# A two-layer streaming encoder step: an earlier selection of the tile whose gates are added in DRAM, and 94 blocks of scores made ahead instead of 82

## The chip, the core and the metric

The kernel runs on one core of one Trainium2 chip. The metric is the device time of one execution in microseconds (us); the kernel before took 4004.89 us, the median of three runs from 3994.92 to 4011.67. Engines are named as in the profile: PE is TensorE's matmul, PEld its weight load, DVE is VectorE, ACT ScalarE, POOL GpSimd, SP SyncE. SP issues the plain transfers and POOL the indirect ones.

## The reference

One inference step of two layers over 640 tokens: 512 of a prompt and 128 of running streams (the sample). Each layer is a token mixer followed by an expert retrieval (PEER) with 16384 experts, each a row of a table `u` and of a table `v`. Per block of 128 tokens:

```python
q = (xb @ w_query).reshape(TB, 8, 2, 128)
s = einsum('thpd,hpkd->thpk', q, keys)
sv, si = top_k(s, 16)
cand = sv[:, :, 0, :, None] + sv[:, :, 1, None, :]
cv, ci = top_k(cand.reshape(TB, 8, 256), 16)
gate = softmax(cv)
act = gelu(einsum('thkd,td->thk', u_tab[idx], xb), approximate=False)
y = einsum('thk,thkd->td', gate * act, v_tab[idx])
```

So each token meets 8 x 16 = 128 experts; `idx` is the expert's row, `gate` its weight.

## The kernel before, in words

The kernel does the retrieval in two ways. The **sparse** way (`sparse_peer`, L852) gathers the 128 chosen rows of `u` and then of `v` for 128 tokens, one row per token and gather, by 256 indirect transfers from POOL (L880, L913), and reduces them on DVE (L884, L920). In each layer it serves the sample and the first of the prompt's four tiles of 128 tokens (the first tile, `GT`). The **dense** way (`dense_peer`, L974) serves the other three tiles, 384 tokens: it makes the scores of all 16384 experts in 128 blocks of 128 experts, multiplies them with a matrix of gates that is zero where an expert was not chosen, and adds up `v`. A block has two halves on PE: 24 matmuls of 384 columns for its scores (8 chunks of the model dimension, 3 products of split float32) and 18 matmuls of 512 columns that combine the gated scores with `v` (L1122, in `combine`). Gelu is on ACT (L996, L1101), the product with the gates on DVE (L1110).

Since the gates are known late, some scores are made ahead: `ahead` (L985) loads a block of `u` (tile `wraw`, L272 in `halves`, two buffers), splits it on ACT and DVE (`whi` L240, `wlo` L241), multiplies, and stores the scores after gelu in DRAM (`sd`, L997). They are the last blocks: with 82 made ahead the loop makes the scores of blocks 0 to 45 itself (L284, in `product2`) and reads those of 46 to 127 back from `sd` (L1096).

The gates of the three tiles come about in two ways. For two tiles `found` (L999) builds them from one-hot matrices on DVE, ACT and PE (L1017 to L1046) and stores them to DRAM as `gd` (L1049), 4 pieces a tile. For the other one, in layer 1 only, `spread` (L1052) adds them in DRAM, into a zeroed array `gz`, by 128 indirect transfers (L1070) of 128 elements each, in 8 groups of 16. In front of each group and behind the last stands a small memset on POOL (`stone`, L1063), the fence: it waits until all 16 transfers of the group before have landed. The loop reads `gz` four blocks at a time (`gch`, L1105), and this load waits for the last fence; it stands in SP's queue with all other plain transfers.

What is selected for a tile is worked out by `select` (L805): some 60 DVE operations from `cand` (L815) over the top 16 to the index tile (`idf`, L865, for the first tile; `at0` and `ati`, L1056 to L1059, for the spread tile).

`FE[l]` holds three numbers for layer l: how many blocks are made ahead during the routing (12), how many at each of the 8 pieces of `found`, and how many in all. The program's order is that of the code at the end of the main function (L1239 to L1275); `de` is the generator of the dense way, and each `next(de)` runs it to its next `yield`. A scheduler then sets each engine's own order from the program and a simulated time line, so a moved piece of code moves rows on all engines.

Of the kernel before, what the change touches and what calls it, by code (L numbers as in the profile page):

```python
# [24 lines left out]
GM, GR, GS = ((4,),(1,)*40+(2,)*60), (8,8), (8,8)  # L25
# [20 lines left out]
SUM = dict(s=(None, "xn"), t=("vm", "vm"))  # L46
KQ = (-1, -1)
SC = (0, 1)
FE = ((12, 5, 72), (12, 8, 82))


class Group:
# [10 lines left out]
def kernel(ctx: ExitStack, tc: tile.TileContext, t: dict):  # L63
# [12 lines left out]
    def tl(tag, shape, dt=F32, name=None):  # L76
        return sb.tile(shape, dt, name=name or tag, tag=tag, bufs=BUFS.get(tag, 1))
# [7 lines left out]
    def gps(who):  # L85
        turn[who] = turn.get(who, -1) + 1
        return bank(banks[who][turn[who] % len(banks[who])])
# [85 lines left out]
    def cleared():  # L173

        while mark[0] is None:
            yield 1
        after(V.memset(zero, 0.0))
        flat = gz.rearrange("g p k t -> (g p k t)").rearrange("(p r c) -> p r c", p=128, c=256)
        for i in range(0, 64, 16):
            fills.append(Y.dma_start(flat[:, i:i + 16], zero[:, None].to_broadcast([128, 16, 256])))  # L180
            for _ in range(6):
                yield 1
# [669 lines left out]
    def sparse_peer(G, l, xhl, sv, si, quad, acc=None):  # L852


        who = G.name
        xn = tl("xn", [128, 1024], name="xnn")
        for hf in range(2):
            p = gps(who)
            for u in range(4):
                for v in range(2):  # L860
                    T.matmul(p[:, 128 * u:128 * u + 128], xhl(v, 4 * hf + u), identr, start=(v == 0), stop=(v == 1))
            S.activation(xn[:, 512 * hf:512 * hf + 512], p, AF.Copy)
        k1, k2, gate = select(who, sv, si, quad)
        idf = tl("idf", [128, 128])
        V.scalar_tensor_tensor(idf, k1, 128.0, k2, op0=OP.mult, op1=OP.add)  # L865
        idt = None
        if acc is None:
            tp = gps(who)[:, :128]
            T.transpose(tp, idf, ident)
            idt = tl("bt", [128, 128], I32, name="idt")  # L870
            V.tensor_copy(idt, tp)
        yield 1
        idx = tl("bi", [128, 128], I32, name="idx")
        after(V.tensor_copy(idx, idf))  # L874
        w = tl("wact", [128, 128])
        rows = []
        for s in range(128 + LG):
            if s < 128:
                rows.append(tl("g", [128, 1024], name="gu"))
                P.indirect_dma_start(out=rows[s], out_offset=None, in_=t["u"][l],  # L880
                                     in_offset=bass.IndirectOffsetOnAxis(ap=idx[:, s:s + 1], axis=0))
            if s >= LG:
                g = rows[s - LG]
                d = V.tensor_tensor_reduce(out=g, in0=g, in1=xn, scale=1.0, scalar=0.0, op0=OP.mult, op1=OP.add,  # L884
                                           accum_out=w[:, s - LG:s - LG + 1])
                if paced[0] == 2:
                    after(d, 4 - s % 4)
                elif s % 4 == 0 and paced[0]:
                    after(d)
            yield 1  # L890
        S.activation(w, w, AF.Gelu)
        V.tensor_tensor(w, w, gate, op=OP.mult)
        if acc is not None:
            yield from weighted(G, l, idx, w, acc)
        else:
            yield from multiplied(G, l, idt, w)
# [77 lines left out]
    def dense_peer(l, xhl, sv, si):  # L974

        G = GA
        n = G.n
        FIRST, EACH, NA = FE[l]
        AHEAD = list(range(128 - NA, 128))
# [176 lines left out]
    def after(ins, back=0):  # L1156

        m = marks[-back] if back and len(marks) >= back else mark[0]
        if m is not None:
            tc.add_manual_dep(ins.ins, m.ins.name, mybir.DependencyInfo(  # L1160
                mybir.DependencyClass.NoSync, mybir.DependencyReason.SCHED_ONLY), reason="order")
# [3 lines left out]
    def gather(n):  # L1165
        for _ in range(n):
            at = tc.cur_priority
            tc.cur_priority = at + later[0]
            while gathers:
                try:  # L1170
                    next(gathers[0])
                    break
                except StopIteration:
                    gathers.pop(0)
            tc.cur_priority = at
# [18 lines left out]
    def mixer_p(l):  # L1194
        if l == 0:
            mixt = [tl("v4", [128, 2, 512], name=f"mix{i}") for i in range(4)]
            yield from even_p(mixt)
        else:
            yield from hgrn(GP, GsP([tl("v4", [128, 2, 512], name=f"gs{i}") for i in range(4)]))
# [10 lines left out]
    for l in range(2):  # L1210
        if l:
            tg["p"].update(sq="w3", r="ge", v="ge", a="g8")
            banks.update(WB)
        order = iter(ORDER[l])
        clears = cleared() if SC[l] else iter(())
        mp = mixer_p(l)
        mk, mark[0], paced[0] = 0, None, THR[0]
        later[0] = LW[l]
        while True:
            w = next(order, "P")  # L1220
            next(clears, None)
            if w == "S":
                if cs is not None:
                    next(cs, None)
                continue
            if next(mp, None) is None:
                break
            if gathers:
                gather(GM[l][mk % len(GM[l])])
                mk += 1  # L1230
                if l and mk == PS:
                    banks["p"] = ["y0", "y1", "s"]
        for _ in clears:
            pass
        for _ in cs or ():
            pass
        paced[0] = False
        later[0] = LATER
        xhl = rmsnorm(GP, 1 + 2 * l)  # L1239
        banks.update({"p": ["y0", "y1", "y2", "y3"], "a": ["y0", "y1", "y2", "y3"], "h": ["s", "y5"]})  # L1240
        sv, si = tl("v4", [128, 4, 16, 16], name="sv"), tl("w3", [128, 4, 16, 16], U16, name="si")
        xa = lambda v, k, xhl=xhl: xhl(v, k)[:, 128:512]
        xt = lambda v, k, xhl=xhl: xhl(v, k)[:, 0:128]
        de = dense_peer(l, xa, sv[:, 1:4], si[:, 1:4])
        for i, _ in enumerate(route_p(l, xhl, sv, si)):
            if i < FE[l][0]:
                next(de)
            gather(GR[l])
        spt = sparse_peer(GT, l, xt, sv[:, 0], si[:, 0], "v4", SUM["t"][l])
        next(spt)  # L1250
        if KT[l] < 0:
            gathers.append(spt)
        for i in range(12 - 4 * SC[l]):
            next(de)
            if i == KQ[l]:
                gathers.append(spt)
            gather(GS[l])
        mark[0], paced[0] = None, THR[1 + l]
        marks.clear()
        later[0] = LD[l]  # L1260
        if l == 0:
            banks.update({"s": ["s"], "u": ['b']})
            tg["s"] = dict(w=[SW1], sq="sq", r="pa", v="pb", a="idf", x="pa")
            cs = chain_s(1)
        for k, _ in enumerate(de):
            if k == KT[l]:
                gathers.append(spt)
            if l or gathers and (gathers[0] is spt or cs is not None):
                gather(PACE[l][k % len(PACE[l])])
            if l == 0 and cs is not None and k >= K0:  # L1270
                if spt not in gathers:
                    tg["s"]["w"] = SW2
                    banks["s"] = SB2
                    if late and next(late[0], None) is None:
                        late.pop(0)  # L1275
                for _ in range(SN[k % len(SN)]):
                    if cs is not None and next(cs, None) is None:
                        cs = None
        if l == 0:
            while late:  # L1280
                for _ in late.pop(0):
                    pass
            for _ in cs or ():
                pass
            cs = None
        paced[0] = False
        later[0] = LATER
        while gathers and (l or gathers[0] is spt):
            gather(1)
# [78 lines left out]
```

## Time and profile before

| | |
|---|---|
| runs before, median (lowest to highest) | 4004.89 us (3994.92 to 4011.67) |
| profiled execution, its own time | 4018.61 us |
| its span in the profile | 4016.7 us |
| busy share PE, PEld, DVE, ACT, POOL | 89%, 73%, 80%, 41%, 40% |
| chain that ended last, by engine | PE 22%, DVE 12%, DMA 10%, POOL 6% |
| transfers over the span | 1097.66 MB, 273 GB/s |

A profile is one execution. Views of it name a group of equal instructions by line, engine and tiles (out<-in), with count and times in microseconds from the span's start. Layer 1's routing ends near 2870 us; the pieces of `found` and the blocks ahead run until 3219 us, the dense loop of layer 1 from 3272 us to the end.

### The profile page before, as it was taken

The page shows a single profiled execution, that of the slowest core. Times are in us where ns is not written, and L with a number is a line of the kernel's source. Part 1 is how long each engine was busy: PE and PEld are TensorE (multiplying, and loading weights), DVE is VectorE, ACT ScalarE, POOL GpSimd, SP SyncE. Part 2 cuts the span into 40 slices and gives each one's busy share as a digit, 9 for nine tenths or more (in the row PEclk, how much of TensorE's full clock was granted, in tenths as well). Part 3 has the DMA queues.
Part 4 walks back from the last instruction along what each step waited for, and adds up shares of the span by engine and source line. Part 5 has one row for each costly group of instructions (what it writes and reads, how often), then busy time and mean ns, then how long its engine had stood idle before and what let it go on. Part 6 is the DMA issues. An engine that isn't in the chain of part 4 may idle for free.

```text
span 4016.7 us, 51334 instructions
## 1 busy us (share of the span) xinstructions
PE 3567.8 (89%) x17676; PEld 2921.1 (73%) x17676; DVE 3217.4 (80%) x6206; ACT 1655.5 (41%) x2717; POOL 1596.2 (40%) x1173
## 2 busy tenths in 40 slices
PE   6978778999999999788998878787999949999998
PEld 4756666789779997556775555566999949998776
DVE  5558999886568879887679877899998738788898
ACT  6644222467633334334444333231348913333333
POOL 0001665431245555541003553564057764444443
PEclk8989899999999999999999777798999979999999
DMA  4334998886789999998665765688457769999999
GB/s 147 113 110 160 328 338 322 317 326 241 264 298 336 338 333 357 370 362 304 227 230 216 258 235 186 225 321 296 140 164 211 211 177 343 334 337 356 385 385 331
DMA packets 480134, 1097.66 MB, mean 273 GB/s; under 512 B 55537, under 2 KB 260337, under 8 KB 474737
## 3 DMA queue, kind: packets, MB, share of 16 engines
q1 hardware_dynamic: 313984, 557.38, 39.7%
q0 software_dynamic: 165888, 537.01, 37.9%
q8 instruction: 139, 2.28, 0.2%
q14 instruction: 123, 1.00, 0.1%
HBM read 1005.92 MB, written 89.23 MB: 273 GB/s over the span
## 4 chain that ended last, share of the span: by engine, by line
PE 22%; DVE 12%; DMA 10%; POOL 6%; issue 5%; ACT 1%; SPq 0%; DVEq 0%; POOLq 0%; ACTq 0%
PE py L1122 10%; POOL gz L1070 5%; DMA ge<-sd 4%; DMA gu<-u,idx 3%; PE ps L284 2%; DVE wlo L241 2%; DVE yv L920 2%; PE pb L284 2%; PE py L291 1%; PE py L292 1%; PE py L293 1%; DMA gz<-gatea,ati 1%; DVE gu L884 1%; PE ps L312 1%; DMA wraw<-v 1%
## 5 line engine op out<-in xcount | busy, mean ns | idle before, releaser
L240 ACT ACTIVATE whi<-wraw 128x1024 fp32r<-128x1024 f32 x710 | 741.3, 1054 | 1024.5 <-PE py L292 307.6
L241 DVE TENSOR_TENSOR wlo<-wraw,whi 128x1024 fp32r<-128x1024 f32 x710 | 862.0, 1217 | 315.1 <-ACT whi L240 124.9
L880 POOL DMA_INDIRECT gu<-u,idx x512 | 670.4, 1309 | 1028.5 <-DVE idx L874 380.1
L1122 PE MATMUL py<-whi,wt 128*128 128x512 f32 x3072 | 798.8, 405 | 107.4 <-ACT wt L240 90.6
L1122 PEld LDWEIGHTS py<-whi,wt 128*128 128x128 f32 x3072 | 581.5, 192 | 258.9 <-ACT wt L240 102.3
L913 POOL DMA_INDIRECT gv<-v,idx x384 | 522.0, 1359 | 540.6 <-DVE yv L920 357.0
L884 DVE CUSTOM_DVE_ANT_0 gu<-gu,xnn 128x1024 f32<-128x1024 f32 x512 | 616.2, 1218 | 58.2 <-DMA gu<-u,idx 57.0
L291 PE MATMUL py<-xhl,whi 128*128 128x512 f32 (+1 forms) x1344 | 522.5, 389 | 74.5 <-ACT xhl L240 30.8
L293 PE MATMUL py<-xhl,wlo 128*128 128x512 f32 (+1 forms) x1344 | 515.9, 385 | 26.6 <-DVE wlo L241 26.3
L292 PE MATMUL py<-xhl,whi 128*128 128x512 f32 (+1 forms) x1344 | 514.1, 382 | 11.1 <-DVE xhl L241 11.0
L920 DVE SCALAR_TENSOR_TENSOR yv<-gv,wact,yv 128x1024 f32<-128x1024 f32 x381 | 486.7, 1277 | 2.7
L1122 PE MATMUL py<-wlo,wt 128*128 128x512 f32 x1536 | 401.6, 393 | 0.7 <-DVE wlo L241 0.7
L291 PE MATMUL ps<-xhl,whi 128*128 128x384 f32 (+1 forms) x1120 | 387.2, 346 | 7.9 <-ACT sm L510 3.7
L293 PE MATMUL ps<-xhl,wlo 128*128 128x384 f32 (+1 forms) x1120 | 388.5, 347 | 3.6 <-DVE wlo L241 3.4
L292 PE MATMUL ps<-xhl,whi 128*128 128x384 f32 (+1 forms) x1120 | 385.1, 344 | 0.0
L291 PEld LDWEIGHTS py<-xhl,whi 128*128 128x128 f32 x1344 | 264.6, 197 | 133.7 <-ACT xhl L240 35.1
L1122 PEld LDWEIGHTS py<-wlo,wt 128*128 128x128 f32 x1536 | 288.6, 188 | 67.6 <-DVE wlo L241 1.3
L1070 POOL DMA_INDIRECT gz<-gatea,ati x128 | 249.2, 1947 | 202.6 <-DVE mr L771 162.1
L293 PEld LDWEIGHTS py<-xhl,wlo 128*128 128x128 f32 x1344 | 264.4, 197 | 84.9 <-DVE wlo L241 37.7
L292 PEld LDWEIGHTS py<-xhl,whi 128*128 128x128 f32 x1344 | 264.8, 197 | 46.8 <-DVE xhl L241 15.1
L944 POOL DMA_INDIRECT gv<-v,idt x128 | 151.7, 1185 | 324.5 <-PE pb L962 296.3
L291 PEld LDWEIGHTS ps<-xhl,whi 128*128 128x128 f32 x1120 | 213.9, 191 | 21.3 <-ACT ge L996 5.8
(444 smaller groups left out, 4947.0 us busy)
## 6 DMA issues: line engine op xcount, KB each, us to landing
wraw<-uT SPq DMA_DIRECT2D x256, 512.0 KB
wraw<-v SPq DMA_DIRECT2D x256, 512.0 KB
wraw<-w SPq DMA_DIRECT2D x98, 512.0 KB
gd<-st SPq DMA_DIRECT2D x40, 1024.0 KB
wraw<-wq SPq DMA_DIRECT2D x64, 512.0 KB
sd<-ge SPq DMA_DIRECT2D x154, 192.0 KB
gch<-gd SPq DMA_DIRECT2D x32, 768.0 KB
ge<-sd SPq DMA_DIRECT2D x114, 192.0 KB
```

The lines of the kernel that those rows point to most:

```text
L240: S.activation(hi, src, AF.Copy)
L241: return V.tensor_tensor(lo, src, hi.bitcast(F32), op=OP.subtract)
L284: m = T.matmul(p, w[wv][:, k], xhl(xv, k), start=(k == 0 and xv == wv), stop=(k == 7 and wv == 1))
L291: T.matmul(p, w[0][:, k], xhl(0, k), start=(k == 0), stop=False)
L292: T.matmul(p, w[0][:, k], xhl(1, k), start=False, stop=False)
L293: T.matmul(p, w[1][:, k], xhl(0, k), start=False, stop=(k == 7))
L880: P.indirect_dma_start(out=rows[s], out_offset=None, in_=t["u"][l], in_offset=bass.IndirectOffsetOnAxis(ap=idx[:, s:s + 1], axis=0))
L884: d = V.tensor_tensor_reduce(out=g, in0=g, in1=xn, scale=1.0, scalar=0.0, op0=OP.mult, op1=OP.add, accum_out=w[:, s - LG:s - LG + 1])
L913: P.indirect_dma_start(out=rows[s], out_offset=None, in_=t["v"][l], in_offset=bass.IndirectOffsetOnAxis(ap=idx[:, s:s + 1], axis=0))
L920: d = V.scalar_tensor_tensor(y, rows[e], w[:, e:e + 1], y, op0=OP.mult, op1=OP.add)
L1070: d = P.indirect_dma_start(out=flat, out_offset=bass.IndirectOffsetOnAxis(ap=ati[:, j:j + 1], axis=0), in_=gate[:, j:j + 1], in_offset=Non ...
L1122: mult[1] = T.matmul(yp[a][hf], wt[:, wv, 128 * a:128 * a + 128], vh[vv][:, 512 * hf:512 * hf + 512], start=(k == 0 and wv == 0 and vv == ...
```

## The change

In layer 1 the generator `de` is run once more in front of `sparse_peer` for the first tile, so `spread` (its selection and 128 indirect transfers) and the first piece of `found` now stand in the program ahead of the first tile's selection; the loop behind has one step less. The middle number of `FE[1]` goes from 8 to 10 and the last from 82 to 94: at the 8 pieces 10 blocks each are made ahead, the last call makes the 2 that are left, and the dense loop makes the scores of 34 blocks itself instead of 46.

```diff
-FE = ((12, 5, 72), (12, 8, 82))
+FE = ((12, 5, 72), (12, 10, 94))
...
             gather(GR[l])
+        if SC[l]:
+            next(de)
+            gather(GS[l])
         spt = sparse_peer(GT, l, xt, sv[:, 0], si[:, 0], "v4", SUM["t"][l])
         next(spt)
         if KT[l] < 0:
             gathers.append(spt)
-        for i in range(12 - 4 * SC[l]):
+        for i in range(12 - 5 * SC[l]):
             next(de)
```

Up to the first selection behind the routing all engines' orders are the same as before. From there they differ. On DVE before, the spread tile's indices (`at`, `ati`) stand behind two whole selections, some 60 rows behind the first tile's `idf`:

```order
L769 MAX_INDEX ci<-cv,cand 128x8 x7
L241 TENSOR_TENSOR wlo<-wraw,whi 128x1024
L865 SCALAR_TENSOR_TENSOR idf<-kf 128x128
L772 MAX cv<-mr 128x8
L773 MAX_INDEX ci<-cv,mr 128x8
```

With the change the same place, behind one selection, has the spread tile's indices, and `idf` comes some 150 rows later, among the one-hot matrices:

```order
L769 MAX_INDEX ci<-cv,cand 128x8 x7
L241 TENSOR_TENSOR wlo<-wraw,whi 128x1024
L1056 SCALAR_TENSOR_TENSOR at_22049<-kf 128x128
L772 MAX cv<-mr 128x8
L1057 TENSOR_SCALAR at_22049<-at_22049,place 128x128
L773 MAX_INDEX ci<-cv,mr 128x8
L1059 CAST ati<-at_22049 128x128
```

Counted from the same first row of that selection, 18 rows `wlo` stand ahead of `idf` in the order before and 20 ahead of `at` in the new one.

On SP before, the first load of `gz` stands behind everything that is made ahead, all of `gd`, and five of the loop's own blocks of `u`:

```order
L997 DMA sd<-ge 128x384
L272 DMA wraw<-uT 128x1024
L1049 DMA gd<-st_25503 128x2048
L1049 DMA gd<-st_25504 128x2048
L272 DMA wraw<-uT 128x1024
L1105 DMA gch<-gz 128x4x128
L1107 DMA gch<-gd 128x8x128
L272 DMA wraw<-v 128x1024
```

With the change it stands behind the load of the 88th block ahead and the store of the 84th; 6 loads and 10 stores of blocks ahead, and the loop's first loads of `u`, come behind it:

```order
L997 DMA sd<-ge 128x384
L272 DMA wraw<-uT 128x1024
L1105 DMA gch<-gz 128x4x128
L1107 DMA gch<-gd 128x8x128
L997 DMA sd<-ge 128x384
L1105 DMA gch<-gz 128x4x128
L272 DMA wraw<-uT 128x1024
L1107 DMA gch<-gd 128x8x128
L997 DMA sd<-ge 128x384
L272 DMA wraw<-uT 128x1024
```

PE's order in both has the scores of the loop's blocks 0, 1 and 2 behind the last block ahead and then the first `combine`. At the program's end DVE before has four sums of gathered rows (`yv`, L920) behind the last block's split, ahead of the closing additions:

```order
L920 SCALAR_TENSOR_TENSOR yv<-gv,wact,yv 128x1024 x4
L901 TENSOR_TENSOR xp<-xp,pb 128x4x128
L1149 TENSOR_TENSOR xp<-xp,py_32293 128x4x128
L1149 TENSOR_TENSOR xp<-xp,py_32302 128x4x128
L901 TENSOR_TENSOR xp<-xp,pb 128x4x128
```

With the change five stand there, and 13 more between and behind the additions of the dense tiles (L1149), ahead of the sparse tile's own (L901):

```order
L920 SCALAR_TENSOR_TENSOR yv<-gv,wact,yv 128x1024 x5
L1149 TENSOR_TENSOR xp<-xp,py_32329 128x4x128
L1149 TENSOR_TENSOR xp<-xp,py_32338 128x4x128
L920 SCALAR_TENSOR_TENSOR yv<-gv,wact,yv 128x1024
L1149 TENSOR_TENSOR xp<-xp,py_32347 128x4x128
L1149 TENSOR_TENSOR xp<-xp,py_32356 128x4x128
L1149 TENSOR_TENSOR xp<-xp,py_32365 128x4x128
L1149 TENSOR_TENSOR xp<-xp,py_32374 128x4x128
L920 SCALAR_TENSOR_TENSOR yv<-gv,wact,yv 128x1024 x12
L901 TENSOR_TENSOR xp<-xp,pb 128x4x128 x2
```

## Rows read from the trace of the kernel before

**Rows 1.** Busy time in stretches: start:end, length, PE, PEld, DVE, ACT, POOL, PEclk, DMA.
```profile
2960.00:2980.00 20.00, 19.66 (x111) 18.77 (x111) 19.86 (x37) 9.68 (x14) 17.26 (x10) 1.00 0.70 158
...
3100.00:3120.00 20.00, 20.00 (x135) 19.93 (x134) 14.34 (x14) 16.47 (x42) 16.62 (x9) 1.00 0.79 224
...
3220.00:3240.00 20.00, 0.00 (x0) 0.00 (x0) 0.00 (x0) 0.00 (x0) 15.21 (x12) 0.56 0.18 0
```

**Rows 2.** DVE in order of time: start, length, engine, line, operation.
```profile
2862.93 0.67 DVE L815 TENSOR_TENSOR cand<-sv 128x512 f32<-128x512 f32 x1
...
2911.31 1.20 DVE L241 TENSOR_TENSOR wlo<-wraw,whi 128x1024 fp32r<-128x1024 f32 x1
2912.43 0.28 DVE L865 SCALAR_TENSOR_TENSOR idf<-kf 128x128 f32<-128x128 f32 x1
...
2950.92 0.29 DVE L1056 SCALAR_TENSOR_TENSOR at<-kf 128x128 f32<-128x128 f32 x1
```

**Rows 3.** POOL in order of time: first scatter, five of eight fences, one late scatter.
```profile
2952.24 2.58 POOL L1070 DMA_INDIRECT gz<-gatea,ati  x1 [162.14 <-DVE mr L771]
...
3035.74 0.09 POOL L1063 MEMSET stone<- 1x1 f32 x1 [5.29 <-DMA gz<-gatea,ati]
...
3082.68 0.09 POOL L1063 MEMSET stone<- 1x1 f32 x1 [3.54 <-DMA gz<-gatea,ati]
...
3199.35 0.09 POOL L1063 MEMSET stone<- 1x1 f32 x1 [2.85 <-DMA gz<-gatea,ati]
...
3233.46 0.09 POOL L1063 MEMSET stone<- 1x1 f32 x1 [1.49 <-DMA gz<-gatea,ati]
...
3234.11 1.55 POOL L1070 DMA_INDIRECT gz<-gatea,ati  x1 [0.56 <-issue]
...
3265.03 0.09 POOL L1063 MEMSET stone<- 1x1 f32 x1 [1.60 <-DMA gz<-gatea,ati]
```

**Rows 4.** SP in order of time, the two issues on either side of the gap.
```profile
3211.21 0.33 SPq L272 DMA_DIRECT2D wraw<-uT  x1
3265.14 0.37 SPq L1105 DMA_DIRECT2D gch<-gz  x1
```

**Rows 5.** ACT in order of time, its last two operations ahead of the gap.
```profile
3218.05 1.06 ACT L240 ACTIVATE whi<-wraw 128x1024 fp32r<-128x1024 f32 x1 [3.50 <-DMA wraw<-uT]
3219.01 0.47 ACT L1101 ACTIVATE ge<-ps 128x384 f32<-128x384 f32 x1
```

**Rows 6.** DVE in order of time, its first operation behind the gap.
```profile
3270.56 0.56 DVE L1110 TENSOR_TENSOR ge<-ge,gch 128x384 f32<-128x384 f32 x1 [51.11 <-DMA gch<-gd]
```

**Rows 7.** The chain that ended last, in order of time: start, length, what.
```profile
3271.73 6.79 PE py L1122 x18
...
3600.67 4.18 PE ps L284 x24
3604.85 4.18 PE py L1122 x18
...
3638.29 35.98 PE py L1122 x156
```

**Rows 8.** Busy time of L1122 alone (PE, PEld), PEclk, DMA share, GB/s, two stretches.
```profile
3271.70:3638.30 366.60, 198.86 (x793) 149.65 (x794) 0.99 0.95 340
3638.30:4005.20 366.90, 355.00 (x1512) 281.86 (x1511) 1.00 1.01 372
```

**Rows 9.** Transfers of the stretch 3638 to 4005 us.
```profile
q0 software_dynamic: 17577, 64.00, 45.2%
...
gv<-v,idx POOLq DMA_INDIRECT x122
```

**Rows 10.** All engines in order of time, the program's end.
```profile
4000.35 5.24 DVE L920 SCALAR_TENSOR_TENSOR yv<-gv,wact,yv 128x1024 f32<-128x1024 f32 x4
...
4003.63 1.54 PE L1122 MATMUL py<-wlo,wt 128*128 128x512 f32 x6
...
4008.74 2.47 DVE L1149 TENSOR_TENSOR xp<-xp,py 128x512 f32<-128x512 f32 x4
```

## The prediction

> **What bounds the kernel now.** I read the busy time by stretches first. Until 3219 us PE is busy all the time, although the one-hot pieces load DVE and ACT as well; then it does nothing for some 50 us, and neither do DVE and ACT, while POOL goes on [rows 1]. What POOL does there is the adding of gates in DRAM: its first scatter starts at 2952.2 and the last fence passes at 3265.0, so the scatter takes 312.8 us [rows 3]. SP shows who waits for it: between 3211.2 and 3265.1 it issues nothing, then the load of `gz` [rows 4]. DVE's next operation, 51 us late, is the product with the gates that this load brings, at 3270.6 [rows 6], and the first `combine` starts at 3271.7 [rows 7]. At 3219.0 ACT had the third block of scores of the loop, the last work for which PE lacked nothing [rows 5]. So the scatter bounds this place.
>
> Behind it the chain alternates between 24 matmuls of scores and 18 of `combine`, 4.18 us each, as long as the loop makes scores itself; from 3638.3 on only `combine` is left [rows 7]. In the first part, 366.6 us, 793 of the 2304 `combine` matmuls are done (44 blocks of 18) with PE never idle; in the second, 366.9 us, 1512 (84 blocks), 4.37 us each, at 372 GB/s with the transfers always busy [rows 8, 9]. PE bounds the first part, the transfers just about the second: 4.37 against the 4.18 that PE needs.
>
> **The change part by part.**
>
> *The selection moves.* The first tile's selection starts at 2862.9 and its `idf` at 2912.4; the spread tile's `at` starts at 2950.9 [rows 2]. In the new order `at` takes the place of `idf` with two more rows `wlo` ahead, 2 x 1.2 us: 2914.8. That is 36.1 us earlier, and the first scatter falls from 2952.2 to 2916.1. No work vanishes: the first tile's selection goes in among the one-hots, where DVE is busy 14.3 us of 20 instead of 19.9 [rows 1], and nothing waits for `idf` before the loop. I cost that at nothing; without that room it would be the same 36 us on DVE.
>
> *The scatter's length.* It isn't constant. The first three groups end at 3082.7, 43.5 us each, beside a DVE that is nearly always busy; the first six at 3199.4, 41.2 each; the seventh took 34.1 and the eighth 31.6, half and wholly beside idle engines, where a scatter took 1.55 us [rows 3]. In the new program PE, and so DVE, run on until about 3231 (below), so I take seven groups at 41.2 and one at 34.1: 322.4 us, nearest to what DVE's load will be. The last fence then passes at 2916.1 + 322.4 = 3238.5. The bounds: 308 us (fence at 3224), near the present length, and 46.9 us a group (375 us), the longest group seen, the third, from 3035.7 to 3082.7 [rows 3].
>
> *Twelve more blocks ahead, and a queue.* If all of them went ahead of the fence they would fill the gap: 12 x 4.18 = 50 us. The new order forbids that: SP meets the load of `gz` when it has issued only 88 of 94 loads, and it is an in-order queue that stood for 54 us on this very load [rows 4]. What is queued behind is what PE needs: six blocks ahead, then three of the loop's. PE has the 82 old blocks and three of the loop's done at 3219.0; in their place it can do 88 by 3219.0 + 3 x 4.18 = 3231.5. Then it stands until the fence, and some more: from the fence to the first DVE work on the loaded gates it was 5.5 us [rows 3, 6]; now a load of `u` of 0.5 MB comes behind these loads (1.4 us at 372 GB/s) and its split on ACT (1.1 us [rows 5]), 8.0 in all. Bounds: 3 us, if the `u` load overtakes, and 10. PE starts again at 3246.5, an idle time of 15 us in place of 53. Nine blocks follow, 9 x 4.18 = 37.6 us (load and store of one, 0.7 MB in 4.18 us, are 170 GB/s, which fits beside what ran at the end of the old stage: DMA busy 0.79 with the same blocks in it [rows 1]), and the first `combine` starts at 3284.1 instead of 3271.7: **12.4 us later**. If the fence came before PE needs the 89th block, it would be 3219.0 + 12 x 4.18 = 3269.2, 2.5 us earlier.
>
> *The loop.* Twelve blocks leave the first part, 12 x (4.18 + 4.18) = 100.3 us, and join the second, 12 x 4.37 = 52.4 us: **47.9 us less**. Their 12 transfers of 512 KB of `u` become 192 KB of stored scores. This end holds if the second part keeps its mix of 1.5 gathers a block. The other end goes by bytes: the loop moved 366.6 x 340 + 366.9 x 372 = 261 MB [rows 8], now 4 MB less; at the old rates the first part, 266 us, moves 90.6 MB and the other 166.5 MB take 447.6 us, 20 us less in all, with the end of the gathers in it.
>
> *The end.* POOL's gathers for the first tile are spread over the loop. Before, the last four sums end with the last `combine`, at 4005.2 [rows 10]. In the new order 13 sums are left then. A gather is 64.00 MB / 122 = 0.52 MB, 1.4 us at 372 GB/s [rows 9], above DVE's 5.24 / 4 = 1.3 us [rows 10]: 17.8 us, then the sparse tile's additions, 2.5 us, where 6.0 us passed from `combine`'s end to DVE's last operation (4008.7 + 2.5 [rows 10]): **14.3 us more**. Bounds: 13.5 at DVE's 1.3 us, and 35 at the 3.0 us a gather that the second part shows (366.9 / 122).
>
> **Sum:** +12.4 - 47.9 + 14.3 = -21.2 us. The profiled execution, 4018.6, would become 3997.4. It lies 13.7 us above the median of the runs shown, so against that: 4004.9 - 21.2 = **3984 us**, 0.5% less. About 0.5%, 20 us, is what a measurement of this kernel can tell from no change, so the forecast sits on that line.
>
> **The rivals.** In all of them the time is the fence's place plus 45.6 us for the restart and nine blocks, and the loop's -33.6 us; a fence at 3259.7 would be no gain.
>
> *The queue doesn't bite.* If the scatter keeps to 308 us, the fence is there before PE's 89th block. For it: before, it took only 312.8. Against: two of these groups had idle engines beside them, and that idleness goes. Then -2.5 - 33.6 = -36 us: 3969.
>
> *The early start is eaten up.* The scatter slows down beside DVE, by the first three groups' 43.5 us: 348 us, fence at 3264, where it was; the change then doesn't do what it says. -21.2 + 25.6 = +4 us: 4009. For it: just these groups ran where the new scatter starts, and single scatters of 2 to 2.6 us beside 1.55 [rows 3]. Against: groups four to six took 38.9 on average, beside a DVE that was busy 72% in one stretch of theirs [rows 1, 3]. The Trainium skill's "Trainium Architecture — The Big Picture", section "What this means for kernel authors", says that the one pair contending on the engines' side of SBUF is DVE and GpSimd, by an exclusive lock and not a shared bandwidth. By it every group beside busy two-input work would cost like the first three, which is this rival's time; the trace agrees that scatters are shortest beside an idle DVE, but shows shares, not a lock.
>
> *The queue bites harder.* Place: SP, the load of `gz` ahead of nine blocks of `u`. If all eight groups take 46.9 us, the fence is at 3291, the first `combine` at 3337, and the sum +31 us: 4036. It is slower by 20 us from a fence at 3279.7 on, 45.4 us a group. For it: a group did take that; against: one of eight.
>
> **How the numbers follow.** The forecast, a fence between some 3228 and 3252: 0.58. The queue doesn't bite: 0.15. Eaten up: 0.18. Bites harder: 0.09. The forecast's own range, with the loop by bytes and the end's bounds, is 3972 to 4000, about half of it on either side of the 20 us; I put 0.33 of its 0.58 on the faster side, since PE's waits in the second part are small. Faster by over 0.5%: 0.33 + 0.15 = 0.48. Within 0.5%: 0.25 + 0.18, and a hundredth of the slow case: 0.44. Slower: 0.08. The range takes in the case without the queue's wait, with a few us for a shorter end, and the eaten-up case to its middle: 3962 to 4010, leaving out the slow case and half of the eaten-up one.
>
> **What would show it.** In the new profile: the first scatter near 2916 and the last fence near 3238; SP without an issue from about 3219 to the fence, then loads of `u`; PE idle for about 15 us once, with nine blocks of scores between that and the first `combine` near 3284; the last of the loop's own scores some 259 us behind it; 96 `combine` at 4.4 us; a dozen sums of gathered rows behind the last `combine`. A fence later than 3265, PE idle in the one-hot pieces, or a `combine` above 4.6 us in the second part would make it wrong.

## The result, and the profile after

The changed kernel takes 4120.24 us (median of four runs, 4112.6 to 4122.45) beside 4002.99 us of the kernel before on the same chip (four runs): a ratio of 1.0289, 95% interval 1.0263 to 1.0315. The forecast was 3984 us, at most 4010. It is wrong in sign and by far more than its range, so the first question is where 117 us come from.

Cut at the same four places, the two profiled executions say in which stage to look (times in us; the last column is what the prediction's steps amount to):

| | before | after | predicted |
|---|---|---|---|
| first scatter starts | 2952.2 | 2903.5 | 2916.1 |
| last fence | 3265.0 | 3208.4 | 3238.5 |
| first `combine` starts | 3271.7 | 3397.4 | 3284.1 |
| from there to the last scores of the loop | 366.6 | 262.9 | 266.3 |
| from there to the last `combine` | 366.9 | 425.1 | 419.3 |
| from there to the span's end | 11.5 | 30.8 | 25.8 |
| span | 4016.7 | 4116.1 | 3995.5 |

The fence is 57 us earlier than before and the first `combine` 126 us later. The loop itself does what was predicted, within 6 us. (The profiled execution of the kernel before took 13.7 us more than its median, as the prediction says; so whatever is set beside its span looks better than it is, and a gain is measured by the ratio of medians.) The busy time of after in the stretches that answer to [rows 1] (columns as there) shows what is between:

```profile
3060.00:3080.00 20.00, 18.92 (x120) 18.21 (x118) 13.49 (x13) 11.21 (x27) 17.56 (x9) 1.00 0.78 209
3080.00:3100.00 20.00, 0.00 (x0) 0.00 (x0) 0.00 (x0) 0.00 (x0) 15.05 (x12) 0.58 0.18 0
...
3180.00:3200.00 20.00, 0.00 (x0) 0.00 (x0) 0.00 (x0) 0.00 (x0) 16.65 (x12) 0.50 0.20 0
...
3220.00:3240.00 20.00, 20.00 (x134) 20.00 (x133) 14.72 (x14) 19.11 (x51) 0.00 (x0) 1.00 0.38 135
```

Again there is a hole, of the same look as the old one [rows 1], which was some 50 us wide; this one is some 130 us wide, and it lies in front of work that before was done in time: half of the one-hot pieces and their blocks. PE, DVE and ACT all stand and POOL alone scatters. ACT in order of time (start, length, and in brackets the idle time before and what ended it) tells who stood first:

```profile
3072.28 0.26 ACT L1006 ACTIVATE tr<-py 128x128 f32<-128x128 f32 x1
3072.69 1.06 ACT L240 ACTIVATE whi<-wraw 128x1024 fp32r<-128x1024 f32 x1
3073.65 0.47 ACT L996 ACTIVATE ge<-py 128x384 f32<-128x384 f32 x1
3208.35 0.28 ACT L1006 ACTIVATE tr<-py 128x128 f32<-128x128 f32 x1 [134.22 <-DMA gz<-gatea,ati]
```

```profile
3208.38 0.09 POOL L1063 MEMSET stone<- 1x1 f32 x1 [1.59 <-DMA gz<-gatea,ati]
```

The ACT row at 3208.35 is the copy of the second transposed matrix of the last tile in `found`, which has nothing to do with the scatter's result; yet a scatter ended its wait, and the last fence, POOL's row, passes at 3208.38, in the same instant. The view of the scatter's own line says the same from the other side:

```profile
L1070 POOL DMA_INDIRECT gz<-gatea,ati x128: 1546/1547/8037, 2903.5 to 3205.2; - x128
...
  ACT tr L1006: 134.2, 1
  POOL stone L1063: 12.7, 8
```

Everything else stands behind this copy: DVE's one-hot (L1017) reads it, and PE, whose next transpose and products wait for ACT and DVE, and SP, whose next store is the one-hot pieces':

```profile
3208.66 1.23 DVE L1017 TENSOR_TENSOR ohb<-iota,tr 128x1024 f32<-128x1024 f32 x1 [133.65 <-ACT tr L1006]
```

```profile
3075.04 0.33 SPq L272 DMA_DIRECT2D wraw<-uT  x1
3210.19 0.80 SPq L1049 DMA_DIRECT2D gd<-st  x2
```

So SP does have a gap, as in [rows 4], but no load of `gz` ends it: that load is issued at 3347.1, 139 us after the fence, and the queue on which the prediction spent most of its care never bites here.

**Why the copy waits.** `tr`, `at` and `ati` share the five buffers of one tag, "ai" (L1005, L1055, L1058). The scatters read their offsets from `ati`, and in the program its buffer counts as free only when the last of the 128 has landed. In the new program the second `tr` of the last tile was given that buffer; in the one before none of layer 1's ten `tr` was. The buffers are handed out by the scheduler on its simulated time line. The orders of the two programs, with the semaphores that each instruction waits for, show it (before, then after; the eight DMASW are POOL's transfers):

```
2001 L1006 ACTIVATE tr_24206<-py1_24204 128x128 [waits PE_49]

1983 L1006 ACTIVATE tr_24478<-py1_24476 128x128 [waits DMASW4_49,DMASW3_49,DMASW5_49,DMASW2_49,DMASW6_49,DMASW1_49,DMASW7_49,DMASW0_49,PE_49]
```

The traces bear this out: before, no copy into `tr` in layer 1 waits for a transfer of POOL's; after, this one alone waits for all eight. That the shared buffer is the cause is so far only argued; that is the theory (W): a wait for a buffer, brought in by the move through the allocation, in no line of the diff. The rivals: the order does it, whatever buffer is used (O); or twelve more blocks are too much for the one-hot stretch.

### The profile page after: what moved, and what is told of

Its sections match the earlier page's. It is cut to its first block, busy times and chain, and to the rows that moved or that the text cites. A ratio compares the mean times of both kernels' runs of the same rounds, so it can differ in the third digit from the quotient of the medians.

```text
span 4116.1 us, 51437 instructions
## 1 busy us (share of the span) xinstructions
PE 3559.5 (86%) x17676; PEld 2914.1 (71%) x17676; DVE 3217.1 (78%) x6206; ACT 1656.3 (40%) x2717; POOL 1600.2 (39%) x1173
## 5 line engine op out<-in xcount | busy, mean ns | idle before, releaser
L1122 PE MATMUL py<-whi,wt 128*128 128x512 f32 x3072 | 794.6, 404 | 56.7 <-ACT wt L240 49.4
L1122 PEld LDWEIGHTS py<-whi,wt 128*128 128x128 f32 x3072 | 577.3, 191 | 211.8 <-ACT wt L240 66.9
L913 POOL DMA_INDIRECT gv<-v,idx x384 | 510.7, 1330 | 528.0 <-DVE yv L920 353.5
L291 PE MATMUL py<-xhl,whi 128*128 128x512 f32 (+1 forms) x1392 | 538.8, 388 | 71.6 <-ACT xhl L240 31.2
L293 PE MATMUL py<-xhl,wlo 128*128 128x512 f32 (+1 forms) x1392 | 534.5, 385 | 26.5 <-DVE wlo L241 26.2
L292 PE MATMUL py<-xhl,whi 128*128 128x512 f32 (+1 forms) x1392 | 531.0, 381 | 11.2 <-DVE xhl L241 11.1
L920 DVE SCALAR_TENSOR_TENSOR yv<-gv,wact,yv 128x1024 f32<-128x1024 f32 x381 | 488.4, 1282 | 5.0 <-DMA gv<-v,idx 2.0
L291 PE MATMUL ps<-xhl,whi 128*128 128x384 f32 (+1 forms) x1168 | 401.9, 344 | 10.3 <-ACT ge L996 5.3
L293 PE MATMUL ps<-xhl,wlo 128*128 128x384 f32 (+1 forms) x1168 | 402.5, 345 | 5.7 <-DVE wlo L241 5.7
L1122 PE MATMUL py<-wlo,wt 128*128 128x512 f32 x1536 | 401.4, 394 | 0.5 <-DVE wlo L241 0.5
L292 PE MATMUL ps<-xhl,whi 128*128 128x384 f32 (+1 forms) x1168 | 399.3, 342 | 0.0
L291 PEld LDWEIGHTS py<-xhl,whi 128*128 128x128 f32 x1392 | 274.2, 197 | 129.8 <-ACT xhl L240 35.5
L1122 PEld LDWEIGHTS py<-wlo,wt 128*128 128x128 f32 x1536 | 289.0, 189 | 67.1 <-issue 1.2
L293 PEld LDWEIGHTS py<-xhl,wlo 128*128 128x128 f32 x1392 | 274.7, 197 | 83.8 <-DVE wlo L241 37.2
L292 PEld LDWEIGHTS py<-xhl,whi 128*128 128x128 f32 x1392 | 274.4, 197 | 46.7 <-DVE xhl L241 15.3
L944 POOL DMA_INDIRECT gv<-v,idt x128 | 158.0, 1234 | 314.9 <-PE pb L962 286.8
L291 PEld LDWEIGHTS ps<-xhl,whi 128*128 128x128 f32 x1168 | 221.6, 190 | 23.9 <-ACT ge L996 7.6
```

The source lines that it names most:

```text
L291: T.matmul(p, w[0][:, k], xhl(0, k), start=(k == 0), stop=False)
L292: T.matmul(p, w[0][:, k], xhl(1, k), start=False, stop=False)
L293: T.matmul(p, w[1][:, k], xhl(0, k), start=False, stop=(k == 7))
L913: P.indirect_dma_start(out=rows[s], out_offset=None, in_=t["v"][l], in_offset=bass.IndirectOffsetOnAxis(ap=idx[:, s:s + 1], axis=0))
L920: d = V.scalar_tensor_tensor(y, rows[e], w[:, e:e + 1], y, op0=OP.mult, op1=OP.add)
L944: P.indirect_dma_start(out=rows[s], out_offset=None, in_=t["v"][l], in_offset=bass.IndirectOffsetOnAxis(ap=idt[:, tok[s]:tok[s] + 1], axis=0))
```

## The experiments

Each ratio is to runs of the kernel before beside the experiment. There it took 4009.4 to 4010.0 us and not 4003.0; the medians that are expected of the first four runs were worked out from the lower figure and lie some 7 us too low.

**The buffer alone.** The changed kernel, with `ati` in the buffer of an accumulator that is long dead (L600).

```diff
-            ati = tl("ai", [128, 128], I32, name="ati")
+            ati = tl("accs", [128, 128], I32, name="ati")
```

> The changed kernel with one thing undone: the index tile `ati`, which the 128 scatters read, gets a buffer of its own (that of a tile long dead); DVE's, POOL's, SP's and PE's orders stay the same row for row. Theory W (the loss is the wait of ACT's second `tr` of the last one-hot tile for all scatters, since it was given the buffer of `ati`): the 134 us wait goes, PE has no hole near 3080 to 3209. The scatter then runs beside a busy DVE, 8 groups of 41 to 43.5 us from 2903.5, last fence 3231 to 3252; the load of `gz` stands ahead of nine blocks, so first `combine` 45.6 us behind the fence, 3277 to 3297; from there to the span's end the changed kernel took 718.7 us, so the span is 3996 to 4016, a median of 3982 to 4002 us. Theory O (the order does it: the one-hot pieces or SP's queue stand behind the scatter whatever buffer it has): as the changed kernel, 4110 to 4125 us, hole in the same place. In between (some 4050) would mean that the wait was only one of two.

Measured: 4005.57 us, ratio to before 0.9989 (0.9978 to 0.9999). The ratio falls from 1.0289 to 0.9989: the whole loss is gone. The copies follow each other, and no scatter is waited for but by the fences:

```profile
3081.14 0.28 ACT L1006 ACTIVATE tr<-py 128x128 f32<-128x128 f32 x1 [1.10 <-PE py L1004]
3083.00 0.27 ACT L1006 ACTIVATE tr<-py 128x128 f32<-128x128 f32 x1
```

The rows of DVE, POOL and SP stand in the same order as in the changed kernel; ACT's differ by one neighbouring pair, 128 us ahead of the hole. So theory O is out. Fence, first `combine` (3287.7) and span (4005.6) lie where W had them; the median is 4 us above W's range, less than the 7 us by which that range was set too low. From this copy to the first `combine` the kernel after took 3397.4 - 3208.4 = 189.0 us, this one 3287.7 - 3083.0 = 204.7: with the hole, the scatter was over when the work went on, and the later wait for the fence fell away. So a copy that starts 125.4 us earlier brings the first `combine` only 109.6 us forward: of the 15.7 us between, PE's wait behind the load of `gz` is 9.7 and the slow restart behind it 3.0 (both below); the rest stays open.

**The control.** The same line in the kernel before.

> Control: the kernel before with `ati` in a buffer of its own. Before, no `tr` waited for the scatter, so theory W gives no change: 3995 to 4012 us, the fence at about 3265, the first `combine` at about 3272. If a buffer of its own helps by itself (fewer waits in the group of five buffers), it would be over 20 us faster and the first run says less than it seems to.

Measured: 4009.67 us, ratio 0.9992 (0.998 to 1.0004), fence at 3260.6, first `combine` at 3267.4. The buffer helps only where it was shared.

**The halves.** First the blocks without the move, then the move without the blocks, both with `ati` in "ai".

```diff
-FE = ((12, 5, 72), (12, 8, 82))
+FE = ((12, 5, 72), (12, 10, 94))
```

> Half of the change alone: 94 blocks ahead, the selection not moved. In its order no `tr` waits for a scatter, and the first load of `gz` stands behind all but three loads of the blocks ahead. Theory W: no hole of 130 us. The scatter starts where it did, 2952, and runs beside busy engines to 3265 to 3290; PE is through the blocks ahead of the load at about 3240 and idle until the fence, then six blocks (25 us) and 8 us of restart: first `combine` 3298 to 3323, then 718.7 us to the span's end: 4017 to 4042, medians 4003 to 4028 us. A rival that lays the loss to the twelve more blocks (PE, ACT or DVE overloaded beside the one-hots): 4080 us or more.

Measured: 4026.78 us, ratio 1.004 (1.0024 to 1.0056), fence 3262.7, first `combine` 3307.4. PE is idle for 35.9 us, its blocks of `u` standing behind the load of `gz`:

```profile
3271.51 0.69 PE L291 MATMUL py<-xhl,whi 128*128 128x384 f32 x1 [35.89 <-ACT whi L240]
```

As W expected; the blocks don't make the hole.

```diff
+        if SC[l]:
+            next(de)
+            gather(GS[l])
...
-        for i in range(12 - 4 * SC[l]):
+        for i in range(12 - 5 * SC[l]):
```

> The other half alone: the selection moved, 82 blocks ahead. Its order has the same wait of the second `tr` of the last tile for the scatters. Theory W: ACT, DVE and PE stand for about 130 us from some 3060 on; PE's work up to the loop, which ended at 3219, ends at about 3349, first `combine` there, 77 us later than before, and the loop as before: 4070 to 4100 us with up to 19 us more at the end. If the hole needs the twelve blocks too, it is 3970 to 4005 us.

Measured: 4102.26 us, ratio 1.0229 (1.0207 to 1.0251), 2 us above W's range, first `combine` at 3357.2, 8 us later than expected. The move alone has the wait, on the same copy, of the same size:

```profile
3216.91 0.28 ACT L1006 ACTIVATE tr<-py 128x128 f32<-128x128 f32 x1 [134.51 <-DMA gz<-gatea,ati]
```

**The queue.** With the hole gone the steps of the prediction can be tried one by one. In the kernel with its own buffer SP does stand at the load of `gz`, and PE behind it:

```profile
3222.73 0.72 SPq L272 DMA_DIRECT2D wraw<-uT  x1
3238.22 0.37 SPq L1105 DMA_DIRECT2D gch<-gz  x1
```

```profile
3247.13 0.69 PE L291 MATMUL ps<-xhl,whi 128*128 128x384 f32 x1 [9.71 <-ACT whi L240]
```

The next run takes the first two loads of `gz` off SP (own buffer kept):

```diff
-                    behind(Y.dma_start(gch[k // 4][:, 0:4], gz[:, :, k:k + 4, :].rearrange("g p k t -> p g k t")), fences[-1:])
+                    behind((P if k < 8 else Y).dma_start(gch[k // 4][:, 0:4], gz[:, :, k:k + 4, :].rearrange("g p k t -> p g k t")), fences[-1:])
```

> The changed kernel with `ati` in a buffer of its own, and the first two loads of `gz` issued by POOL instead of SP; ACT's and PE's orders stay. With its own buffer alone PE stood about 10 us between 3237 and 3248 and the first `combine` began at 3287.7. Theory Q (SP, standing at the load of `gz`, holds the loads of blocks of `u` behind it): SP never stands, the 10 us of idle PE go, first `combine` 3276 to 3279 with the fence still near 3238, the rest as it was: a span of 3994 to 3997, a median of about 3995 us. Rival (PE stands there for the split of the blocks or for ACT, or the restart is only moved): first `combine` still 3285 or later, 4003 to 4008 us.

Measured: 3991.56 us, ratio 0.9949 (0.993 to 0.9967) beside 0.9989 with the buffer alone. First `combine` at 3280.0, 7.8 us earlier; after 3077 us no idle time of PE over 0.7 us is left in front of it. SP goes on loading past the fence, at 3233.2, which POOL waits for by itself:

```profile
3226.65 0.82 SPq L272 DMA_DIRECT2D wraw<-uT  x1
3228.39 0.37 SPq L1107 DMA_DIRECT2D gch<-gd  x1
...
3232.79 1.90 SPq L272 DMA_DIRECT2D wraw<-uT  x1
...
3236.97 0.33 SPq L272 DMA_DIRECT2D wraw<-uT  x1
```

Theory Q holds: SP, standing at the load of `gz`, held the blocks back. Its size needs care, since executions reach this stage at different times: the first selection starts between 2854.6 and 2867.1 in the eight profiles with the move. Counted from there, the first `combine` comes 12.1 us earlier than with the buffer alone, about the 9.7 us of idle time and the 3.0 us of slow restart. The ratios differ by 16 us, with some 8 us of uncertainty.

**The third corner.** Move and own buffer with 82 blocks, `gz` loaded by SP.

> The selection moved and `ati` in a buffer of its own, but 82 blocks ahead as before: the third corner of the pair. In its order the load of `gz` stands ahead of two blocks ahead and three of the loop. PE is through 80 blocks at about 3204 (88 were done at 3237 with 94), stands until the fence, 3230 to 3238, then 8 us of restart and five blocks, 21 us: first `combine` 3259 to 3267 (before 3271.7); the loop as before, 733.5 us, and 12 to 16 us at the end: a span of 4005 to 4016, medians 3998 to 4010 us, so 0 to 12 us faster than before. If moving the selection frees what the fence is earlier (27 us), 3983 us; if the twelve blocks were what keeps the change from losing, 4015 us or more.

Measured: 4010.93 us, ratio 0.9997 (0.9984 to 1.001), 1 us above the range; first `combine` at 3265.7, in the range. An early fence (3233.4, 32 us earlier than before) by itself brings nothing that can be told: the load of `gz` now stands ahead of five blocks, and PE waits 44.7 us for them:

```profile
3242.78 0.69 PE L291 MATMUL ps<-xhl,whi 128*128 128x384 f32 x1 [44.68 <-ACT whi L240]
```

**A version that beats both.** Move, own buffer, `gz` loaded by POOL, and as many blocks as PE can do until the fence: 85.

```diff
-FE = ((12, 5, 72), (12, 8, 82))
+FE = ((12, 5, 72), (12, 8, 85))
```

> Selection moved, own buffer, POOL loads the first two pieces of `gz`, 85 blocks ahead: as many as PE can do until the fence. With three blocks of the loop these are 88, done at about 3237; fence 3235 to 3239, product with the gates 5 us later, first `combine` 3243 to 3248. First part: three blocks less than before, 366.6 - 3 x 8.4 = 341.5; second 366.9 + 3 x 4.4 = 380; the end 11.5 to 16: a span of 3976 to 3985, 32 to 41 us less than before's, medians 3967 to 3978 us if theories W and Q are both right. If POOL's loads come late or the loop gives it back, 3990 us or more.

Measured: 3984.73 us, ratio 0.9937 (0.9918 to 0.9956). It is the fastest of the study. The median is 7 us above the expectation, though the profiled span, 3977.8, lies in its range: the expectation counts from the span before, and that execution took 4018.6 us where the median is 4010.0 here. First `combine` at 3237.5, first part 340.7, second 388.0, end 11.6: the second part is 8 us longer than expected, 4.46 us a block, and the first `combine` 5.5 us earlier. PE hardly waits for the gates any more; of the hole of 53 us in front of the first `combine` there is left:

```profile
3237.47 5.28 PE L1122 MATMUL py<-whi,wt 128*128 128x512 f32 x12 [5.98 <-ACT wt L240]
```

**More blocks than fit** (the same with `(12, 9, 88)` for layer 1).

> As the run with 85 blocks ahead, a buffer of its own and POOL's loads of `gz`, but with 88 ahead. Past the number that fits in front of the fence a block ahead should be worth nothing: it puts off the first `combine` by 4.2 us and saves 4.2 us of scores later, and the blocks of the second part cost 4.42 to 4.46 instead of 4.18. First `combine` near 3250, first part 315, second 400, end 12 to 16: a span of 3977 to 3983, medians 3980 to 3992 us, equal to 85 blocks or up to 5 us slower. If blocks ahead gain also behind the fence, 3975 us or less.

Measured: 3985.93 us, ratio 0.994 (0.9927 to 0.9952): no different. First `combine` 3256.6, first part 314.9, second 407.6. In these two runs a block ahead is worth something only while PE would otherwise stand.

**Without the move** (92 blocks, own buffer, POOL's loads).

> The selection not moved, `ati` in a buffer of its own, POOL loads the first two pieces of `gz`, 92 blocks ahead, as many as fit in front of the later fence (3261 to 3265): is the move worth anything once the queue is out of the way? PE is through 88 blocks at about 3235 as in the run with the blocks alone, through 95 with the three of the loop at 3264; first `combine` 3266 to 3272, first part 283, second 415, end about 27: a span of 3991 to 3997, a median 12 to 20 us above the run with 85 blocks and the move, some 3997 to 4005 us. If the move gives nothing, both are within 5 us.

Measured: 4000.32 us, ratio 0.9974 (0.9964 to 0.9985), with the fence at 3264.4 and the first `combine` at 3269.7. Against the runs with the move, at 85 and 88 blocks, the move is worth 14 to 15 us once neither the buffer nor the queue takes it back. But the number of blocks is not quite fitted here: PE stands 12.8 us in front of the first `combine`, where it stood 6.0 with 85 blocks and the move, so by estimate up to 7 us (12.8 - 6.0) may be that, and not the move. No run tells which.

```profile
3269.73 5.49 PE L1122 MATMUL py<-whi,wt 128*128 128x512 f32 x12 [12.81 <-ACT wt L240]
```

**The end.** The changed kernel with its own buffer, and faster gathers:

```diff
-PACE = ((4,4,4,0)*10+(4,)*90,(3,))
+PACE = ((4,4,4,0)*10+(4,)*90,(4,))
```

> The changed kernel with `ati` in a buffer of its own, and the first tile's gathers stepped 4 and not 3 at each block of the loop: 5 fewer sums of gathered rows stand behind the last `combine` in its order. With the buffer alone the end (last `combine` to the end) took 30.8 us. If the end's length is the sums left over, at 1.45 us each as in the changed kernel's end, it is 23 to 24 us; the second part of the loop moves the same rows in the same time, so a median of 3997 to 4002 us. If the second part is bound by transfers, what is taken from the end is given back there, and the time stays at 4003 to 4008 us.

Measured: 4005.78 us, ratio 0.9985 (0.9971 to 0.9999), as the buffer alone. The end is 23.9 us instead of 30.8, and the second part 429.1 instead of 424.4, the first 265.1 instead of 262.7: what the end loses the loop gets back, as the second theory said. Up to the loop its program is that of the run with the buffer alone; yet the fence came at 3244.9 and PE stood 15.7 us:

```profile
3254.43 0.69 PE L291 MATMUL ps<-xhl,whi 128*128 128x384 f32 x1 [15.70 <-ACT whi L240]
```

## Why the prediction was wrong, step by step

The run with the buffer alone has the prediction's program in the sense in which the prediction meant it, without the wait; so it shows which steps were right, and by how much.

| | predicted | after | own buffer |
|---|---|---|---|
| first `combine` against before | +12.4 | +125.6 | +16.0 |
| loop, first part | -100.3 | -103.7 | -103.9 |
| loop, second part | +52.4 | +58.2 | +57.5 |
| end | +14.3 | +19.3 | +19.3 |
| sum, against a span of 4016.7 | -21.2 | +99.4 | -11.1 |

- **The failed step** is the first, "The selection moves": "No work vanishes", "nothing waits for `idf`", "I cost that at nothing". It asked whether moved rows meet a busy DVE and whether anyone needs the first tile's indices. It did not ask which buffers the moved tiles hold, and for how long. The runs put a wait of 134 us on ACT in its place: 134.2 after, 134.5 with the move alone, none with `ati` elsewhere. No rival had it; the one that ended slower placed its loss on SP and could lose 31 us at most. The new order, with its waits, had the row above before anything had run; the prediction took only the rows' places from it.
- **The scatter's start and length.** The start was put at 2916.1; it was 2903.5 after and 2909.4 with its own buffer. Of this 5.2 us are the working's own: it has 51.9 us from the selection's start to `at`, and in all eight profiles with the move it is 46.7; the rest is when that execution reached the selection. The length was put at 322.4, between 308 and 375: it was 304.8 after, when half of it ran beside idle engines, and 328.7 with its own buffer, so that this fence, 3238.1, fell on the 3238.5 forecast by luck: two errors cancel.
- **The queue.** The mechanism is right, and its size fair: PE idle for 9.7 us (15 forecast, with PE standing from 3231.5; it came there 6 us later), 15.7 in the run with the faster gathers; first `combine` 49.6 us behind the fence (45.6 forecast). The nine blocks took 40.6 us, not 37.6. The working priced them at the full clock; behind PE's idle time the first matmul takes 0.69 us instead of 0.33, and the granted clock is 0.50 there, 1.2 of its 2.4 GHz, 0.67 over the whole stretch. The rows ahead had such a restart: 6.79 us for the first 18 matmuls behind the old hole, 4.18 later [rows 7]. The stretch and two of its 20 us:

```profile
3240.00:3260.00 20.00, 12.62 (x56) 12.12 (x57) 3.94 (x4) 5.89 (x8) 0.00 (x0) 0.67 0.78 254
...
3249.00:3251.00 2.00, 2.00 (x8) 2.00 (x7) 0.49 (x1) 1.06 (x1) 0.00 (x0) 0.50 0.74 191
```

- **The loop and the end.** The first part came out right (262.9 measured; the sum has 266.3, though the prediction's list of signs says 259), the second was put 5 to 6 us too short. The rows that answer to [rows 8] are these (after, second part alone):

```profile
3660.30:4085.30 425.00, 410.10 (x1732) 324.54 (x1730) 0.99 1.03 380
```

  96 blocks in 425 us are 4.43 us each, at 380 GB/s, where 84 took 4.37 at 372. The end was put at 25.8 us and is 30.8. Place and kind were right: the 13 sums are there. But they end 23.8 us behind the last `combine` (4085.3), not 17.8 (13 times 1.4 us would be 18.2), since DVE does six additions of the dense tiles between them (1.28 and 2.48 us) and waits for the last rows; and the sparse tile's two additions, each behind a PE product, take 3.8 us, not 2.5. Behind DVE's last operation it is 3.2 us instead of 5.5:

```profile
4107.78 1.28 DVE L920 SCALAR_TENSOR_TENSOR yv<-gv,wact,yv 128x1024 f32<-128x1024 f32 x1 [0.39 <-DMA gv<-v,idx]
4110.28 0.69 DVE L901 TENSOR_TENSOR xp<-xp,pb 128x512 f32<-128x512 f32 x1 [1.21 <-PE pb L929]
4112.17 0.69 DVE L901 TENSOR_TENSOR xp<-xp,pb 128x512 f32<-128x512 f32 x1 [1.21 <-PE pb L929]
```

- **The rivals.** "The queue doesn't bite" came true after, for a reason that is not in it, and not as a gain. Of "the early start is eaten up" over a third is seen: with its own buffer the last fence is 27 us earlier than before though the start is 43 us earlier. The page's rule under it (the Trainium skill, "Trainium Architecture — The Big Picture", section "What this means for kernel authors": DVE and GpSimd contend for a shared pair of ports, by an exclusive lock) agrees with the trace at one end: four groups beside idle engines took 31.5 us each after. DVE's busy share does not order the others; which operations it does bears on them more, as the last section shows. No run shows a lock as such.

So with the failed step mended the change ends at 0.9989 of the time before, some 4 us less, where the forecast's sum said 0.5%, 21 us. By spans it is 11.1 us less, and the 10 us between the two sums lie in the terms of the table: 5 each in the second part and the end; the 3.6 lost in the restart came back in the first part.

## What to carry to other kernels

When a piece of code moves, list not only who waits for its results but which buffers it holds and until when: here the tile that the transfers read kept its buffer until the last of them had landed, and whoever was given that buffer next waited as if it needed the result. Where a scheduler assigns buffers, compare the waits of the new order on every engine, ACT's too, and read any wait on a transfer that the instruction's own operands don't explain. And where a queue issues in order, a gain in front of it is kept only if the waiting load is taken out of the way of the others: the early fence was worth nothing that can be told until POOL issued its load, then an estimated 8 to 15 us.

## What the runs showed of the hardware

A group of 16 scatters took between 31.5 and 55.4 us over all the runs, more than the 46.9 us that was the bound. With the buffer alone, busy time from fence to fence (columns as in [rows 1]):

```profile
2909.00:2950.00 41.00, 39.95 (x225) 38.25 (x224) 40.16 (x105) 16.78 (x25) 33.90 (x17) 1.00 0.66 161
...
3038.00:3092.60 54.60, 47.61 (x281) 46.07 (x280) 46.34 (x57) 40.54 (x97) 44.10 (x17) 0.94 0.72 222
3092.60:3130.00 37.40, 37.40 (x253) 37.40 (x252) 28.67 (x25) 33.76 (x86) 30.11 (x18) 1.00 0.75 193
```

The longest group is not the one with the busiest DVE: the first has DVE busy 40.16 of 41.00 us, the fourth 46.34 of 54.60. In the fourth two single scatters, one right behind the other, take over 6 us each (a third one takes 5.98):

```profile
3049.02 6.11 POOL L1070 DMA_INDIRECT gz<-gatea,ati  x1 [0.31 <-issue]
3055.44 6.70 POOL L1070 DMA_INDIRECT gz<-gatea,ati  x1 [0.30 <-issue]
3062.44 1.55 POOL L1070 DMA_INDIRECT gz<-gatea,ati  x1 [0.30 <-issue]
```

The same lengths (6.1, 6.7 and 6.0 us, or two of the three) come back in the fourth group of the changed kernel and of four other runs with the move; in two more with it they are absent. DVE in order of time beside the scatter of 6.70 us shows what goes with them:

```profile
3054.95 1.22 DVE L1021 TENSOR_TENSOR e<-iota,tr 128x1024 fp32r<-128x1024 f32 x1
3056.09 2.36 DVE L837 TENSOR_TENSOR oh<-iu,iota 128x1024 f32<-128x1024 uint32 x2
3058.36 1.23 DVE L1024 TENSOR_TENSOR ohh<-ohb,gh 128x1024 fp32r<-128x1024 f32 x1
3059.49 1.23 DVE L241 TENSOR_TENSOR wlo<-wraw,whi 128x1024 fp32r<-128x1024 f32 x1
3060.63 1.22 DVE L841 TENSOR_REDUCE kf<-oh 128x64 f32<-128x1024 f32 x1
```

Operations on two tensors (TENSOR_TENSOR and SCALAR_TENSOR_TENSOR) follow each other without a gap. Summed over this trace, such operations fill 38% of the time of the 50 scatters of 1.55 us, and 87% of the five longest. By group they fill 24.3 of 40.0 us in the first, though DVE is nearly always busy there, 35.4 of 42.7 and 32.8 of 45.9 in the next two, and 40.6 of 54.6 in the fourth. So long scatters go with unbroken rows of such operations. That these make the scatters wait fits, but no run tried it; it stays open.
